# A 32-byte spacer above the right-hand tiles of a two-layer decoder trunk

## The chip, the cores and the metric

The kernel runs on one core of a Trainium2 chip. The metric is the device time of one execution in microseconds (us). A core has a matrix engine (TensorE; PE in the profile, with its weight loads shown apart as PEld), a vector engine (DVE), a scalar engine (ACT), a general engine (POOL), a queue engine (SP) that here issues nearly all transfers, an on-chip memory of 128 partitions (SBUF), and an accumulator memory in banks that the matrix engine writes (PSUM). A matrix multiplication takes two operands from SBUF: the stationary one is loaded into the array first (LDWEIGHTS), the moving one is then streamed through it (MATMUL).

## The reference

A trunk of two layers works on a sequence of 256 tokens with 1024 features, float32. Layer 0 mixes tokens with a gated linear recurrence, layer 1 with sparse attention of 16 heads; after each mixer comes an MLP of width 4096, and before every part a root-mean-square normalisation.

```python
for i in range(DEPTH):                         # DEPTH = 2
    h = _rmsnorm(x, norm_mix[i])
    if i % N_MIXERS == 0:
        x = x + _rglru_mixer(h, rg_w_in[j], ...)
    else:
        x = x + _nsa_mixer(h, nsa_w_in[j], ...)
    h = _rmsnorm(x, norm_ffn[i])
    x = x + _sq_relu_mlp(h, mlp_w_up[i], mlp_w_down[i])   # relu(h @ up)**2 @ down
return _rmsnorm(x, norm_final)
```

Nearly all the arithmetic is in the products with weights: the input and output projections of both mixers and the two MLPs.

## The kernel before

**Layout.** The activations stand transposed: features on the partitions, tokens along a row, in chunks of 128 features by 256 tokens (1024 bytes a partition). `xt` is the residual stream. A weight matrix is cut into pieces of 128 x 1024, which is eight stationary operands of 128 x 128.

**Precision by splitting.** A product in float32 is made of three in the faster type float32r. A weight piece arrives in a `raw` tile; ACT (now and then DVE) writes its rounded high part to a `whi` tile (L278 in the MLPs, L326 in the planned sections), and DVE writes the difference raw minus high to a `wlo` tile (L287 and L323). The activations are split in the same way into pairs: `hhl` holds the normalised input (high and low part of eight chunks), `uhl` the MLP's activations (32 tiles, one for each chunk of 128 of the width 4096), `xbh`/`xbl` the recurrence's output, `oh`/`ol` the attention's. `mm3` (L317 to L320) then does high times high, high times low and low times high into one PSUM bank. The weight is stationary, the activation moves, so each of the three matmuls has its own weight load of 128 x 128 and streams 256 columns.

**Stages.** The recurrence layer (L525 to L764) and the attention layer (L828 to L1247) are planned: a list scheduler in Python (`Plan`) with written costs gives each engine its order of instructions before the kernel is built. The two MLPs (`mlp`, L766 to L819) are written out: 32 up-projections read `hhl` and write `uhl`, 8 down-projections read `uhl`, and `tick` splits later weight pieces in between. In the attention layer the value projection (`values`, L991 to L1021) has it the other way round: `hhl` is stationary there, and `whi`/`wlo` move, in 304 and 256 columns. The scores (L1098, L1099) and the products with the probabilities (L1147, L1162) have small operands of their own.

**Loads.** SP issues the weight pieces in a fixed order into five `raw` tiles, well ahead of the splits; at the start of the recurrence layer two more pieces go to the tile `y`, which is free then (`spare`).

**Where the tiles lie.** SBUF is allocated as two stacks. Most pools grow upward from the left: `consts`, `xres`, `weights` (seven `whi`, seven `wlo`), `stats`, and then the pools of the stage. Three pools take from the right end downward: `hsplit` (the tile `hhl`), then `rawweights` (five `raw` tiles), then, during an MLP, `up0` or `up1` (`uhl`). Every tile is rounded up to a multiple of 32 bytes of a partition. As the program is allocated, `hhl` starts at byte 212960 of each partition, the `raw` tiles at 190560 + 4480 i, the `uhl` tiles 2048 bytes apart from 125024; `whi` starts at 28704 + 4480 i, `wlo` at 60064 + 4480 i. Every one of these is 32 past a multiple of 64, and so are `xbh`, `xbl`, `oh`, `ol`, `warm`, `xt`'s chunks, `t`, `u`, `sa`, `sb`, `kh`, `kl`, and the start of `pT`. Counted in blocks of 128 bytes, `hhl`, `raw`, `uhl`, `xbh`, `xbl`, `oh` and `ol` start at 96, `whi` and `wlo` at 32. Some unused tiles named `edge`, `edge0` and `edge1` (320, 64 and 64 bytes) stand in the left stack and set such positions.

The lines that the change touches are L471 to L475, where the tiles of the constants end and `hhl` is made:

```python
471    consts.tile([P, 80], F32, name="edge")
472    ones = consts.tile([P, 1], F32, name="ones")
473    pool.memset(ones, 1.0)
474    hhl = hpool.tile([P, KC, 2, S], F32R, name="hhl")
475    hh, hl = hhl[:, :, 0], hhl[:, :, 1]
```

Of the kernel before, what the change touches and what calls it, by code (L numbers as in the profile page):

```python
# [12 lines left out]
F32 = mybir.dt.float32  # L13
# [6 lines left out]
P = 128  # L20
# [199 lines left out]
def trunk_kernel(ctx: ExitStack, tc: tile.TileContext, x_in, vec_in, const_in, w2_in, wts, out):  # L220
# [6 lines left out]
    hpool = ctx.enter_context(tc.tile_pool(name="hsplit", bufs=1, side="right"))  # L227
# [243 lines left out]
    consts.tile([P, 80], F32, name="edge")  # L471
    ones = consts.tile([P, 1], F32, name="ones")
    pool.memset(ones, 1.0)
    hhl = hpool.tile([P, KC, 2, S], F32R, name="hhl")
    hh, hl = hhl[:, :, 0], hhl[:, :, 1]  # L475
    acc = spool.tile([P, S], F32, name="acc")
# [921 lines left out]
```

## Time and profile before

| | us |
|---|---|
| device time, median of 3 runs (570.91 to 571.75) | 571.49 |
| device time of the profiled execution | 571.1 |
| its span, first to last instruction | 569.3 |
| PE busy | 560.9 |
| PEld busy | 553.7 |
| DVE busy | 407.0 |
| ACT busy | 342.7 |
| POOL busy | 40.1 |
| mean granted clock of TensorE | 0.996 |

The profiled execution takes 1.8 us more than its span, for what lies before the first and after the last instruction that the profile shows. A MATMUL's busy time in the profile runs from its start to the end of its passage through the array, and the next one starts before that; so the mean of one (some 277 ns) says little, and the distance from start to start, or a count of matmuls in a stretch of time, says how fast they follow each other.

### The profile page before, as it was taken

To read this page: it belongs to the slowest core of one execution; us is meant where nothing else is said; L and a number is where in the kernel's file an instruction comes from. 1 tells how busy PE (TensorE), PEld (TensorE's weight loads), DVE (VectorE), ACT (ScalarE), POOL (GpSimd) and SP (SyncE) were. 2 spreads that over 40 slices of the span, in tenths; PEclk is the share of its full clock that TensorE was granted. 3 is DMA by queue.
4 is the path that set the end of the run, shared out by engine and by line. 5 is a ranking of instruction groups with operands and counts; after the bars stand their busy time and mean duration, and the time that the engine had idled before them with its cause. 6 is when DMAs were issued, how large, how long until landed. Compare 5 with 4: busy or idle time off the path is not lost.

```text
span 569.3 us, 12420 instructions
## 1 busy us (share of the span) xinstructions
PE 560.9 (99%) x4906; PEld 553.7 (97%) x4906; DVE 407.0 (71%) x877; ACT 342.7 (60%) x666; POOL 40.1 (7%) x55
## 2 busy tenths in 40 slices
PE   9999999999999999999999999999999999999995
PEld 8989999999999999999999999999999999999995
DVE  6999989766775664565749999989867775553532
ACT  7799675865664443444456988886865664443410
POOL 1000000000000211221000000000000000222310
PEclk9999999999999999999999999999999999999998
DMA  8936468556657456456685232354676666566402
GB/s 318 407 98 209 121 214 255 184 189 191 195 194 235 155 204 222 163 190 221 212 264 154 65 114 57 112 171 144 198 230 193 191 202 231 156 205 218 126 1 74
DMA packets 33225, 103.66 MB, mean 182 GB/s; under 512 B 3856, under 2 KB 8080, under 8 KB 33168
## 3 DMA queue, kind: packets, MB, share of 16 engines
q1 hardware_dynamic: 32624, 102.42, 55.8%
q8 instruction: 38, 0.62, 0.4%
q10 hardware_dynamic: 544, 0.46, 0.2%
q14 instruction: 19, 0.16, 0.1%
HBM read 99.23 MB, written 1.05 MB: 176 GB/s over the span
## 4 chain that ended last, share of the span: by engine, by line
PE 95%; DVE 2%; issue 1%; DMA 1%; ACT 1%; DVEq 0%; POOL 0%; SPq 0%; ACTq 0%; POOLq 0%
PE bank L318 28%; PE bank L319 27%; PE bank L320 27%; PE bank L1162 3%; PE bank L686 2%; PE bank L1147 2%; PE bank L1098 1%; PE bank L1099 1%; PE bank L567 1%; DMA pt<-tt 1%; PE bank L1005 1%; DVE wlo L323 1%; PE bank L1006 1%; PE bank L1007 1%; ACT whi L326 1%
## 5 line engine op out<-in xcount | busy, mean ns | idle before, releaser
L318 PE MATMUL bank<-hhl,whi 128*128 128x256 f32 x768 | 213.2, 278 | 0.0
L319 PE MATMUL bank<-hhl,whi 128*128 128x256 f32 x768 | 212.4, 277 | 0.0
L320 PE MATMUL bank<-hhl,wlo 128*128 128x256 f32 x768 | 212.2, 276 | 0.0
L287 DVE TENSOR_TENSOR wlo<-raw,whi 128x1024 fp32r<-128x1024 f32 x115 | 143.2, 1266 | 1.9 <-ACT whi L278 1.9
L319 PEld LDWEIGHTS bank<-hhl,whi 128*128 128x128 f32 x768 | 144.3, 188 | 0.3 <-DVE hhl L576 0.2
L318 PEld LDWEIGHTS bank<-hhl,whi 128*128 128x128 f32 x768 | 144.3, 188 | 0.1
L320 PEld LDWEIGHTS bank<-hhl,wlo 128*128 128x128 f32 x768 | 144.2, 188 | 0.0
L318 PE MATMUL bank<-uhl,whi 128*128 128x256 f32 x512 | 141.5, 276 | 0.0
L319 PE MATMUL bank<-uhl,whi 128*128 128x256 f32 x512 | 141.4, 276 | 0.0
L320 PE MATMUL bank<-uhl,wlo 128*128 128x256 f32 x512 | 141.4, 276 | 0.0
L278 ACT CAST whi<-raw 128x1024 fp32r<-128x1024 f32 x116 | 118.1, 1039 | 23.1 <-issue 18.8
L318 PEld LDWEIGHTS bank<-uhl,whi 128*128 128x128 f32 x512 | 96.1, 188 | 0.0
L319 PEld LDWEIGHTS bank<-uhl,whi 128*128 128x128 f32 x512 | 96.1, 188 | 0.0
L320 PEld LDWEIGHTS bank<-uhl,wlo 128*128 128x128 f32 x512 | 96.1, 188 | 0.0
L323 DVE TENSOR_TENSOR wlo<-raw,whi 128x1024 fp32r<-128x1024 f32 (+2 forms) x72 | 77.4, 1091 | 7.0 <-ACT whi L326 6.9
L326 ACT CAST whi<-raw 128x1024 fp32r<-128x1024 f32 (+2 forms) x63 | 60.0, 966 | 21.4 <-PE bank L319 9.1
L522 DVE TENSOR_TENSOR xt<-xt,bank 128x256 f32<-128x256 f32 x39 | 15.9, 418 | 75.8 <-PE bank L320 75.8
L783 ACT ACTIVATE u<-t 128x256 f32<-128x256 f32 x64 | 26.7, 418 | 58.8 <-DVE t L778 58.6
L778 DVE SCALAR_TENSOR_TENSOR t<-bank,rstd 128x256 f32<-128x256 f32 x64 | 26.9, 423 | 39.7 <-PE bank L320 39.5
L1112 ACT ACTIVATE pt<-pt,mx 128x256 f32<-128x256 f32 (+1 forms) x64 | 28.7, 450 | 3.6 <-DVE mx L1109 3.2
L785 DVE TENSOR_TENSOR uhl<-u,uhl 128x256 fp32r<-128x256 f32 x64 | 26.6, 416 | 3.0 <-ACT uhl L784 3.0
L498 ACT ACTIVATE hhl<-xt,vec 128x256 fp32r<-128x256 f32 x8 | 4.1, 510 | 39.4 <-DVE xt L522 39.4
(201 smaller groups left out, 730.5 us busy)
## 6 DMA issues: line engine op xcount, KB each, us to landing
raw<-in_dram SPq DMA_DIRECT2D x171, 512.0 KB, 4.4
raw<-in_dram SPq DMA_DIRECT2D x4, 560.0 KB, 4.7
gw<-in_dram SPq DMA_DIRECT2D x4, 512.0 KB, 8.3
raw<-in_dram SPq DMA_DIRECT2D x6, 256.0 KB, 5.2
y<-in_dram SPq DMA_DIRECT2D x2, 512.0 KB, 6.8
pT<-in_dram SPq DMA_DIRECT2D x2, 512.0 KB, 5.7
xt<-in_dram SPq DMA_DIRECT2D x3, 256.0 KB, 5.2
kh<-kh SPq DMA_DIRECT2D x8, 64.0 KB, 2.8
```

Source lines behind the costliest of these rows:

```text
L278: (act.copy if eng is None else eng.tensor_copy)(hi_t[i % NSPL][:, :n], raw_of(i)[:, :n])
L287: (eng or dve).tensor_tensor(lo[:, :n], raw_of(i)[:, :n], hi[:, :n].bitcast(F32), op=OP.subtract)
L318: pe.matmul(ps, wh, xh, start=start, stop=False)
L319: pe.matmul(ps, wh, xl, start=False, stop=False)
L320: pe.matmul(ps, wl, xh, start=False, stop=stop)
L323: return lambda e: e.tensor_tensor(o, a, h.bitcast(F32), op=OP.subtract)
L326: return lambda e: (e.copy if e is act else e.tensor_copy)(o, a)
L778: dve.scalar_tensor_tensor(t, z, 0.0, rs, op0=OP.max, op1=OP.mult)
L783: act.activation(u, t, AF.Square)
L785: later(lambda: dve.tensor_tensor(ul[m], u, uh[m].bitcast(F32), op=OP.subtract))
L1112: add("act", (0.39, 0.49)[qc], lambda e, row=row, j=j: e.activation(row, row, AF.Exp, bias=mx[:, j:j + 1], scale=-1.0, accum_out=sm[:, j:j ...
L1162: two = lambda c, w, y, **k: [e.matmul(o()[own_(hf), c0 + c.start:c0 + c.stop], w(hf), y(hf), **k) for hf in range(2)]
```

## The change

One tile is added to the pool `hsplit` ahead of `hhl`: 8 float32 values, 32 bytes of each partition, which nothing reads or writes. As the pool takes from the right end downward, the new tile lies above `hhl`, and `hhl`, the five `raw` tiles and the 32 `uhl` tiles of each MLP lie 32 bytes lower: `hhl` at 212928, `raw` at 190528 + 4480 i, `uhl` from 124992, all at multiples of 64 (64 past a multiple of 128). The left stack, with `whi`, `wlo`, `xt`, `xbh`, `xbl`, `oh`, `ol` and all others, does not move. No instruction is added, removed or reordered; the scheduler does not see addresses, so the order on every engine and all waits stay as they are.

```diff
     consts.tile([P, 80], F32, name="edge")
     ones = consts.tile([P, 1], F32, name="ones")
     pool.memset(ones, 1.0)
+    hpool.tile([P, 8], F32, name="edge2")
     hhl = hpool.tile([P, KC, 2, S], F32R, name="hhl")
     hh, hl = hhl[:, :, 0], hhl[:, :, 1]
     acc = spool.tile([P, S], F32, name="acc")
```

## The prediction

> **What bounds the kernel now.** I read the page first: busy times, granted clock, and the chain that ended last by engine and line.
>
> ```profile
> PE 560.9 (99%) x4906; PEld 553.7 (97%) x4906; DVE 407.0 (71%) x877; ACT 342.7 (60%) x666; POOL 40.1 (7%) x55
> PEclk9999999999999999999999999999999999999998
> PE 95%; DVE 2%; issue 1%; DMA 1%; ACT 1%; DVEq 0%; POOL 0%; SPq 0%; ACTq 0%; POOLq 0%
> PE bank L318 28%; PE bank L319 27%; PE bank L320 27%; PE bank L1162 3%; PE bank L686 2%; PE bank L1147 2%; PE bank L1098 1%; PE bank L1099 1%; PE bank L567 1%; DMA pt<-tt 1%; PE bank L1005 1%; DVE wlo L323 1%; PE bank L1006 1%; PE bank L1007 1%; ACT whi L326 1%
> ```
>
> The matrix engine at its full clock is the bound: 82% of the chain are the three lines of `mm3`, 95% some matmul. No wait of it is worth removing; only the pace of the matmuls is. So the next view was the groups by line and shape, for how many of them read a moved tile, then the windows, for their pace in two stretches without a pause. (A windows row: stretch, its length, PE busy with the count, clock, DMA share, GB/s.)
>
> ```profile
> L318 PE MATMUL bank<-hhl,whi 128*128 128x256 f32 x768 | 213.2, 278 | 0.0
> L318 PE MATMUL bank<-uhl,whi 128*128 128x256 f32 x512 | 141.5, 276 | 0.0
> L318 PE MATMUL bank<-oh,whi 128*128 128x256 f32 x64 | 18.4, 288 | 0.0
> L318 PE MATMUL bank<-xbh,whi 128*128 128x256 f32 x64 | 17.7, 276 | 0.0
> ...
> 110.00:210.00 100.00, 100.00 (x883) 1.00 0.62 195
> 400.00:540.00 140.00, 140.00 (x1238) 1.00 0.62 195
> ```
>
> `hhl` moves in 3 x 768 = 2304 matmuls and `uhl` in 3 x 512 = 1536: 3840 of 4906 stream a tile that the change shifts. `oh` and `xbh` stay. A window also counts the matmuls under way at its edge, 0.276 us long, about 2.4 of them; so the pace is 140 / 1235.6 = 0.1133 us from start to start. One nanosecond of it is worth 3.84 us.
>
> What is 113.3 ns made of? The timeline gives the price of a column, where the value projection streams 304 and then 256:
>
> ```profile
> 284.05 0.31 PE L1005 MATMUL bank<-whi,hhl 128*128 128x304 f32 x1
> 284.19 0.30 PE L1006 MATMUL bank<-wlo,hhl 128*128 128x304 f32 x1
> 284.33 0.30 PE L1007 MATMUL bank<-whi,hhl 128*128 128x304 f32 x1
> 284.47 0.28 PE L1005 MATMUL bank<-whi,hhl 128*128 128x256 f32 x1
> 284.59 0.28 PE L1006 MATMUL bank<-wlo,hhl 128*128 128x256 f32 x1
> 284.71 0.28 PE L1007 MATMUL bank<-whi,hhl 128*128 128x256 f32 x1
> ```
>
> Three of 304 take 0.42 us, 140 ns each; two of 256 take 0.24 us, 120 ns each. 20 ns for 48 columns is 0.417 ns a column, 106.7 ns for 256. In the steady stretches a matmul therefore takes 6.6 ns more than its columns, and 6.6 / 0.417 is 16 columns, which is 64 bytes of float32. A row of 1024 bytes that starts 32 past a multiple of 64 touches 17 blocks of 64 bytes; one that starts on a multiple touches 16. 17 x 16 columns x 0.417 ns is 113.3 ns. That is the case for the change.
>
> The other candidate is the weight load, since each matmul has its own. Its pace alone shows where the moving operand is one column wide (L514), and its place in the steady rhythm beside it:
>
> ```profile
> 19.59 0.53 PEld L514 LDWEIGHTS bank<-ones,x 128*128 128x128 f32 x4
> 20.04 0.19 PEld L318 LDWEIGHTS bank<-hhl,whi 128*128 128x128 f32 x1
> 20.15 0.19 PEld L319 LDWEIGHTS bank<-hhl,whi 128*128 128x128 f32 x1
> ...
> 300.34 0.28 PE L318 MATMUL bank<-hhl,whi 128*128 128x256 f32 x1
> 300.35 0.19 PEld L319 LDWEIGHTS bank<-hhl,whi 128*128 128x128 f32 x1
> 300.46 0.28 PE L319 MATMUL bank<-hhl,whi 128*128 128x256 f32 x1
> ```
>
> Five loads start in 20.15 - 19.59 = 0.56 us, 112 ns apiece. In the rhythm a load starts some 0.01 us after a matmul has started, and the next matmul 0.11 us after the load. The load is thus close behind: however fast the stream becomes, the loads alone hold the pace near 112 ns.
>
> Last, the rhythm is not always kept:
>
> ```profile
> 6.09 1.11 PE L567 MATMUL bank<-warm 128*128 128x256 f32 x8
> 7.04 0.28 PE L318 MATMUL bank<-hhl,whi 128*128 128x256 f32 x1
> ...
> 8.42 0.28 PE L318 MATMUL bank<-hhl,whi 128*128 128x256 f32 x1
> ...
> 9.84 0.28 PE L318 MATMUL bank<-hhl,whi 128*128 128x256 f32 x1
> 9.95 0.28 PE L319 MATMUL bank<-hhl,whi 128*128 128x256 f32 x1
> ```
>
> From 8.42 to 9.84 are twelve matmuls, 118 ns each, on the same tiles that later run at 113.3; eight on `warm` take 0.95 us, 119 ns each. Stream and load disturb each other there, and fall into step from 9.84 on. That step is something the change can spoil.
>
> **The change part by part.** No instruction and no wait is added or moved; three kinds of access get another start address.
>
> (1) `hhl` and `uhl` as the moving operand, 3840 matmuls. The bounds: nothing gained if the load holds 113.3 already; at the other end the columns alone, 6.6 ns x 3840 = 25.3 us, which the load's own pace forbids. Between these I take the load's 112 ns, the nearest row: 113.3 - 112 = 1.3 ns, times 3840 = 5.0 us. What is late next is the load, whose tiles `whi` and `wlo` stay where they are. Stretches out of step get no term.
>
> The Trainium skill ("TensorE: Matmul & The Clock Gate", section "Wait — 56ns, not 53.3ns?") puts the warm distance at N / 2.4 GHz plus about 2.5 ns; for 256 columns that is an estimate of 109.2 ns, 4.1 ns under this trace. By it the sum would be 4.1 x 3840 = 15.7 us. The trace's 113.3 ns departs from it, so part of the 6.6 ns is not that fixed cost.
>
> (2) `raw` as a source of the splits, and `hhl`, `uhl` as their target. Price of an element:
>
> ```profile
> L323 DVE TENSOR_TENSOR wlo<-raw,whi 128x1024 fp32r<-128x1024 f32 x56 | 67.7, 1219 | 6.9 <-ACT whi L326 6.9
> L323 DVE TENSOR_TENSOR wlo<-raw,whi 128x256 fp32r<-128x256 f32 x12 | 4.6, 421 | 0.0
> L705 DVE SCALAR_TENSOR_TENSOR t<-a,t 128x512 f32<-128x512 f32 x4 | 2.7, 686 | 0.1
> L702 DVE SCALAR_TENSOR_TENSOR i<-i,xb 128x512 f32<-128x512 f32 x4 | 2.7, 683 | 0.0
> ...
> 263.59 1.03 ACT whi L326
> 283.26 1.22 DVE wlo L323
> ```
>
> (1219 - 421) / 768 = 1.04 ns an element. `a` (L705) lies on a multiple of 64, everything at L702 32 past one: 686 against 683 ns, no gain. I take zero. Were a 64-byte block saved or lost per split it would be 16 x 1.04 = 17 ns; in the MLPs that is hidden by the matmuls, and between 263.6 and 284.5 us (the last two rows, of the chain in order of time), where the chain leaves PE, seven splits stand on it: 0.12 us either way. Without the cover, 180 splits would cost 3 us.
>
> (3) The loads into `raw`, all on SP's queue.
>
> ```profile
> raw<-in_dram SPq DMA_DIRECT2D x171, 512.0 KB, 4.4
> ACT whi L326 <- DMA raw<-in_dram: 4.0, 7, 1.2
> ```
>
> A split waits for a load seven times, 4.0 us in all. One block of 64 in a row of 4096 bytes is 1/64 of 4.4 us, 0.07 us, seven times 0.5 us either way; I take zero, as the same bytes move in the same number of rows.
>
> (4) `hhl` as the stationary operand, 96 matmuls of the value projection, at 120 and 140 ns, not in step: between -5 and +5 ns each, 0.5 us either way, taken as zero.
>
> The sum: 571.1 (the profiled execution) - 5.0 = 566.1. The median of the runs is 0.4 above the profiled one: **566.5 us**.
>
> **The rivals.** *Faster, as above* (A): for it speaks the exact 17 x 16, and that columns are the slope; against it, that the load is so close. Its own range, for a pace between 111.4 and 112.9 ns, is 564 to 570.
>
> *No change* (B): the 113.3 is a closed loop of matmul start, load start, 0.11 us, next matmul start; the moving address has no part in it. The rows at 300.34 to 300.46 fit this as well. For it speaks that the loads at 19.59 are only 1.3 ns faster with almost no stream beside them; against it, that 304 columns take 20 ns longer than 256, so the stream does count. Time: 571.5, with (2) to (4) between 570.4 and 572.6. The Trainium skill ("SBUF — State Buffer", section "Door 1: The DMA port swizzle") gives SBUF lines of 16 bytes; both starts are on such a line and a row has 64 lines either way, so by that rule the result is this one. No row here shows lines of 16.
>
> *Slower* (C): the step is lost. The stream now changes block half a block earlier against the weights, which still start in the middle of one, and the two may meet at the memory in every matmul, as between 8.42 and 9.84. Price 118 - 113.3 = 4.7 ns for each one out of step: it decides from 1.14 us / 4.7 ns = 243 more of them, costs 9.0 us for half of the 3840 (580.5) and 18.0 for all (589.5). For it speaks that the same tiles run at both paces; against it, that every long stretch did find its step.
>
> *Much faster* (D): load and hand-over overlap, so that only the 0.11 us from load to matmul is left, 110 ns: 3.3 x 3840 = 12.7 us, 558.8. Against it the 112 at L514.
>
> **How the numbers follow.** A 0.40, B 0.30, C 0.24, D 0.06. The predicted time is A's. A change of 0.2%, 1.1 us, is about what a measurement of this kernel can tell from none. Faster by more: A and D, 0.46; the same: B, 0.30; slower: C, 0.24. The range goes from 558 (D) to 581 (C with half of the matmuls out of step); left out are C's worse half and what lies below D, about 0.13. A's own range stands above.
>
> **What would show it.** The stretch 110 to 210 holds 883 matmuls: near 893 for A, 883 for B, 848 if C is complete, 909 for D. The distance from load to matmul stays 0.11 us in A and B and grows under C. The loads at L514 stay at 112 ns, DVE's 1219 ns and ACT's splits stay within 20 ns, or (2) was wrong. The prediction is wrong if the pace changes where `oh` or `xbh` stream, which did not move, or if the time changes while the pace in that stretch doesn't.

## The result, and the profile after

| | before | after |
|---|---|---|
| device time, median (range) | 571.50 us (570.91 to 571.75) | **577.73 us** (577.50 to 578.52) |
| runs | 4 | 4 |
| ratio after / before, 95% interval | | 1.0123 (1.0110 to 1.0137) |
| span of the profiled execution | 569.3 us | 575.7 us |
| mean granted clock | 0.996 | 0.997 |

The change makes the kernel 6.2 us slower; 566.5 us, faster, was forecast. Each engine's busy time, the chain by engine, and the group with the most matmuls, of the profile page after:

```profile
PE 567.7 (99%) x4906; PEld 560.9 (97%) x4906; DVE 407.0 (71%) x877; ACT 343.1 (60%) x666; POOL 40.1 (7%) x55
PE 95%; DVE 2%; issue 1%; ACT 1%; DMA 1%; DVEq 0%; POOL 0%; SPq 0%; ACTq 0%; POOLq 0%
L318 PE MATMUL bank<-hhl,whi 128*128 128x256 f32 x768 | 213.1, 277 | 0.0
```

Same counts, same clock, same bound; only PE and its loads (PEld, 553.7 before) are busy longer, by 6.8 and 7.2 us, and a group's busy time hides where. The windows show it. They are laid inside the four MLP stages: up-projections of layer 0, down-projections of layer 0, then the same two of layer 1. Columns: stretch, length, PE busy with the count of matmuls, clock, DMA share, GB/s. Before:

```profile
110.00:170.00 60.00, 60.00 (x531) 1.00 0.62 194
185.00:260.00 75.00, 75.00 (x664) 1.00 0.57 192
410.00:470.00 60.00, 60.00 (x532) 1.00 0.68 207
490.00:555.00 65.00, 65.00 (x576) 1.00 0.45 144
```

and after:

```profile
110.00:170.00 60.00, 60.00 (x532) 1.00 0.64 196
185.00:260.00 75.00, 75.00 (x634) 1.00 0.55 179
410.00:470.00 60.00, 60.00 (x532) 1.00 0.69 209
490.00:555.00 65.00, 65.00 (x553) 1.00 0.49 154
```

With 2.4 taken off each count for the matmuls at the edges, the pace of the up-projections (`hhl` streams) is 113.3 ns before and after (the 531 gives 113.5; one matmul more or less in 60 us is 0.2 ns). The down-projections (`uhl` streams) go from 75 / 661.6 = 113.4 to 75 / 631.6 = 118.7 ns in layer 0 and from 113.3 to 65 / 550.6 = 118.1 ns in layer 1. Times 768 matmuls each that is 4.1 + 3.6 = 7.7 us. The span grew by 6.4; the other 1.3 us are small gains elsewhere, 0.5 of them reached before 20 us (the same load starts at 20.04 us in the prediction's row and at 19.54 after, shown further down) and 0.7 in the attention layer. The timeline of the layer 0 down-projections, PE alone, first before:

```profile
199.72 0.28 PE L319 MATMUL bank<-uhl,whi 128*128 128x256 f32 x1
199.83 0.28 PE L320 MATMUL bank<-uhl,wlo 128*128 128x256 f32 x1
199.95 0.28 PE L318 MATMUL bank<-uhl,whi 128*128 128x256 f32 x1
...
200.74 0.28 PE L319 MATMUL bank<-uhl,whi 128*128 128x256 f32 x1
```

and after:

```profile
199.82 0.28 PE L318 MATMUL bank<-uhl,whi 128*128 128x256 f32 x1
199.94 0.28 PE L319 MATMUL bank<-uhl,whi 128*128 128x256 f32 x1
200.06 0.28 PE L320 MATMUL bank<-uhl,wlo 128*128 128x256 f32 x1
200.18 0.28 PE L318 MATMUL bank<-uhl,whi 128*128 128x256 f32 x1
...
200.89 0.28 PE L318 MATMUL bank<-uhl,whi 128*128 128x256 f32 x1
```

Before, nine matmuls start in 1.02 us, 113 ns each; after, nine in 1.07 us, 119 ns each, all three lines alike. PE is busy throughout both windows. The pace after is the one called out of step in the prediction.

**A premise was wrong.** The text on the change and the prediction say that `hhl` moves. It does not. A right-hand pool ends where the pool before it began, but inside it the tiles are laid upward: the five `raw` tiles lie at 190560 + 4480 i, the first the lowest. By that order `edge2`, made first, takes the low 32 bytes of `hsplit`, 212928 to 212960, and `hhl` stays at 212960. Only the pools to its left, `raw` and `uhl`, lie 32 lower. That `hhl`'s stages keep 113.3 ns to the count agrees, and a run below moves `hhl` itself.

### The profile page after: what moved, and what is told of

It is laid out like the page before. It is cut to its first block, busy times and chain, and to the rows that moved or that the text cites. A ratio compares the mean times of both kernels' runs of the same rounds, so it can differ in the third digit from the quotient of the medians.

```text
span 575.7 us, 12420 instructions
## 1 busy us (share of the span) xinstructions
PE 567.7 (99%) x4906; PEld 560.9 (97%) x4906; DVE 407.0 (71%) x877; ACT 343.1 (60%) x666; POOL 40.1 (7%) x55
## 4 chain that ended last, share of the span: by engine, by line
PE 95%; DVE 2%; issue 1%; ACT 1%; DMA 1%; DVEq 0%; POOL 0%; SPq 0%; ACTq 0%; POOLq 0%
PE bank L318 28%; PE bank L319 27%; PE bank L320 27%; PE bank L1163 3%; PE bank L687 2%; PE bank L1148 2%; PE bank L1099 1%; PE bank L1100 1%; PE bank L568 1%; DMA pt<-tt 1%; PE bank L1006 1%; DVE wlo L323 1%; PE bank L1007 1%; PE bank L1008 1%; ACT whi L326 1%
## 5 line engine op out<-in xcount | busy, mean ns | idle before, releaser
L319 PE MATMUL bank<-uhl,whi 128*128 128x256 f32 x512 | 144.1, 281 | 0.0
L318 PE MATMUL bank<-uhl,whi 128*128 128x256 f32 x512 | 144.0, 281 | 0.0
L320 PE MATMUL bank<-uhl,wlo 128*128 128x256 f32 x512 | 144.0, 281 | 0.0
```

Of the source, the lines that this page charges most:

```text
L318: pe.matmul(ps, wh, xh, start=start, stop=False)
L319: pe.matmul(ps, wh, xl, start=False, stop=False)
L320: pe.matmul(ps, wl, xh, start=False, stop=stop)
```

## The experiments

Three theories stood at first. **Blocks**: the moving row's start decides alone; by the prediction a start on a multiple of 64 is better, by T2 of the expectations it is worse. **T3**: the new place of `raw` disturbs the matmuls. **Distance** (T1, from rival C): what counts is where the moving row starts against the stationary operand, from which the step of stream and load depends. Before, `hhl` and `uhl` start at 96 and the weights at 32 in blocks of 128 bytes, a distance of 64; after, `uhl` stands at 64, a distance of 32. Further runs ask how exact the distance must be, whether the length of the load plays a part, and whether fewer, wider streams escape it. Diffs are against the kernel before unless told otherwise. Kernels with an interval ran several times; the others ran once, beside before.

**Which tile does it.** `uhl_only` moves the activations alone 32 bytes lower, `raw_only` the weights' landing tiles alone (`uhl` then lies 2048 lower than before, a whole number of blocks).

```diff
# uhl_only, in mlp behind the uhl tiles
+            up.tile([P, 8], F32, name="pad")
# raw_only, against the kernel after, behind the uhl tiles
+            up.tile([P, 504], F32, name="pad")
```

> Only uhl lies 32 bytes lower, at 64 past a multiple of 128; raw and hhl lie as before. Theory T1 (what counts is how the start of the moving row stands to the start of the weights): the down-projections lose the step, 118 to 119 ns a matmul against 113.3, the up-projections keep it; 577 to 578 us. T2 (a moving row that starts on a multiple of 64 is slow by itself): the same. T3 (raw's new place makes the splits or loads collide with the matmuls): 571 to 572 us.

> Only raw lies 32 bytes lower; uhl lies 2048 bytes lower than before, so again 96 past a multiple of 128. T1 and T2: as before, 571 to 572 us, every long stretch at 113.3 ns. T3: 577 to 578 us, with the down-projections at 118 to 119 ns.

Measured: `uhl_only` 577.54 us, ratio 1.0125 (1.0108 to 1.0142); `raw_only` 571.03, 1.0007 (0.9996 to 1.0019). The down-projection windows, first of `uhl_only`:

```profile
185.00:260.00 75.00, 75.00 (x634) 1.00 0.55 180
490.00:555.00 65.00, 65.00 (x552) 1.00 0.46 153
```

and of `raw_only`:

```profile
185.00:260.00 75.00, 75.00 (x664) 1.00 0.59 191
490.00:555.00 65.00, 65.00 (x576) 1.00 0.45 146
```

Both pads stand behind the `uhl` tiles in the program; as the tiles of a right-hand pool are laid upward, such a pad lies above them and pushes them down. The 32 bytes by which `uhl` lies lower are the whole loss; `raw` is worth nothing, and T3 falls.

**Row or distance.** `as_described` does what the section on the change says: a spacer behind `hhl`, so that `hhl`, `raw` and `uhl` all lie 32 lower. `all_lower` lowers the left stack by 32 as well, weights included: every operand then starts on a multiple of 64, and the distance is 64 again.

```diff
# as_described
     hhl = hpool.tile([P, KC, 2, S], F32R, name="hhl")
+    hpool.tile([P, 8], F32, name="pad_h")
# all_lower: the same, and
-    consts.tile([P, 80], F32, name="edge")
+    consts.tile([P, 72], F32, name="edge")
```

> hhl, raw and uhl all lie 32 bytes lower: here the normalised input moves too. T1 and T2: the up-projections and the projections of both mixers lose the step as well, up to 2304 more matmuls at 5.4 ns, 585 to 591 us. T3: 577 to 578 us, the up-projections at 113.3 ns. The theory of the prediction (fewer blocks in an aligned row) has the up-projections at 112 ns.

> Everything lies 32 bytes lower, the weights whi and wlo too, so every address of before has lost 32 and all differences are as before; all tiles of the big matmuls start on a multiple of 64. T1: the step is back everywhere, 571 to 572 us at 113.3 ns. T2: all stages are slow, 590 us or more. The theory of blocks: less than 113.3 ns, 560 to 567 us.

Measured: `as_described` 587.81 us, ratio 1.0305 (1.0290 to 1.0321); `all_lower` 570.57, 1.0004 (0.9994 to 1.0013). The windows of `as_described`:

```profile
110.00:170.00 60.00, 60.00 (x508) 1.00 0.55 187
185.00:260.00 75.00, 75.00 (x637) 1.00 0.57 190
410.00:470.00 60.00, 60.00 (x508) 1.00 0.61 187
490.00:555.00 65.00, 65.00 (x553) 1.00 0.57 186
```

and of `all_lower`:

```profile
110.00:170.00 60.00, 60.00 (x532) 1.00 0.58 195
185.00:260.00 75.00, 75.00 (x664) 1.00 0.58 193
410.00:470.00 60.00, 60.00 (x532) 1.00 0.68 203
490.00:555.00 65.00, 65.00 (x576) 1.00 0.43 140
```

With `hhl` moved, its stages fall to 60 / 505.6 = 118.7 ns too. With everything on a multiple of 64 the pace is 113.3 to the count, neither faster nor slower. So the row's own start costs and brings nothing; the theory of blocks falls, both as gain and as loss.

**How exact the distance must be.** Four kernels, with another distance in each stage. `sweep_64_96` lowers `uhl` by 64 in layer 0 and by 96 in layer 1. `weights_96` puts the kernel after's weights 96 higher, so that `uhl` is 64 away from them again and `hhl` 96. `fine_16` and `fine_8` go 16 and 8 bytes to either side of 64.

```diff
# sweep_64_96, behind the uhl tiles
+            up.tile([P, (16, 24)[layer]], F32, name="pad")
# weights_96, against the kernel after, ahead of the first weight tile
+    wpool.tile([P, 24], F32, name="pad_w")
# fine_16; fine_8 has (2, 30)
+            ub = up.tile([P, NF * 2 * S + 32], F32R, name="uhl")
+            uo = (4, 28)[layer]
+            uhl = [ub[:, uo + 2 * S * i:uo + 2 * S * (i + 1)] for i in range(NF)]
```

> From the kernel before: uhl 64 bytes lower in layer 0 (32 past a multiple of 128, the same place in a block of 64 as the weights) and 96 bytes lower in layer 1 (on a multiple of 128). If the relation to the weights repeats every 64 bytes, layer 0's down-projections keep 113.3 to 113.5 ns and layer 1's run at 118 to 119, some 575 us. If it repeats only every 128 bytes, layer 0 loses the step too, 578 us or more.

> From the changed kernel: the weights (and the left tiles above them) lie 96 bytes higher, on a multiple of 128; uhl stays at 64 past one, hhl at 96 past one. T1 (the relation): the down-projections are back at 113.3 to 113.5 ns, since uhl and the weights stand to each other as before, and now the up-projections, with hhl in the middle of a block and the weights at its start, run at 118 to 119; oh and xbh moved with the weights. If the start of the moving row alone counted, down stays at 118 to 119 and up at 113.3.

> From the kernel before: uhl 16 bytes higher in layer 0 and 16 bytes lower in layer 1. If the two streams only have to be in the same half of a block of 64, both layers keep 113.3 to 113.5 ns (571 us); if their starts have to agree exactly, both run at 118 to 119 (578 us). The theory of blocks has no gain here.

> From the kernel before: uhl 8 bytes higher in layer 0 and 8 bytes lower in layer 1. As for 16 bytes: 113.3 to 113.5 ns in both layers if a neighbourhood is enough, 118 to 119 if the starts have to agree exactly; an intermediate pace would say that the loss grows with the distance.

One run each: 579.31, 581.29, 579.14 and 580.49 us beside 570.78 of before. All four windows of `weights_96`, where one kernel holds both cases:

```profile
110.00:170.00 60.00, 60.00 (x506) 1.00 0.55 186
185.00:260.00 75.00, 75.00 (x664) 1.00 0.58 193
410.00:470.00 60.00, 60.00 (x505) 1.00 0.60 186
490.00:555.00 65.00, 65.00 (x576) 1.00 0.52 170
```

The loss has changed sides: the down-projections of the kernel after, with nothing done to `uhl`, are back at 664 and 576, and the up-projections, whose `hhl` did not move, pay. The down-projections of `sweep_64_96` and of `fine_8`:

```profile
185.00:260.00 75.00, 75.00 (x634) 1.00 0.54 178
490.00:555.00 65.00, 65.00 (x550) 1.00 0.49 155
```

```profile
185.00:260.00 75.00, 75.00 (x623) 1.00 0.53 176
490.00:555.00 65.00, 65.00 (x545) 1.00 0.48 154
```

Put together, from these counts (`fine_16` counts 631 and 552 there), less 2.4:

| moving start less stationary start, modulo 128 | where | ns from start to start |
|---|---|---|
| 0 | `sweep_64_96`, layer 0 | 118.7 |
| 32 | after, down, layers 0 and 1; `as_described`, up | 118.7, 118.1; 118.7 |
| 48 | `fine_16`, layer 1 | 118.3 |
| 56 | `fine_8`, layer 1 | 119.8 |
| **64** | before, `raw_only`, `all_lower`; `weights_96`, down | **113.3 to 113.5** |
| 72 | `fine_8`, layer 0 | 120.9 |
| 80 | `fine_16`, layer 0 | 119.3 |
| 96 | `sweep_64_96`, layer 1; `weights_96`, up | 118.7; 119.1, 119.4 |

Of these eight distances the step is kept at 64 alone. It is no slope: eight bytes to either side lose more than 32 do. One thing was not kept apart there: `fine_8`'s rows start at 104 and 120, the only starts here that are no multiple of 16, so the 1.5 to 1.6 ns by which it is slower than `fine_16` may come from the row's own start and not from the distance.

**Does the load's length set the pace?** The prediction held that the loads alone allow no less than 112 ns. `half_load` loads 64 of the 128 weight columns in most down-projections, `quarter_load` 32; the other output features of these chunks are left out. Each keeps the distance of 64 in one layer (`uhl` 128 lower) and has 32 in the other. `half_load`; `quarter_load` has 32 columns and the two pads exchanged:

```diff
# behind the uhl tiles
+            up.tile([P, (32, 8)[layer]], F32, name="pad")
...
-                        mm3(z, wh[:, w], wl[:, w], uh[i], ul[i], i == 0 and not seeded, i == NF - 1)
+                        if seeded or i in (0, NF - 1):
+                            mm3(z, wh[:, w], wl[:, w], uh[i], ul[i], i == 0 and not seeded, i == NF - 1)
+                        else:
+                            c = slice(k * P, k * P + 64)
+                            mm3(z[:64], wh[:, c], wl[:, c], uh[i], ul[i], False, i == NF - 1)
```

> From the kernel before: in the down-projections all but the first and the last of the 32 chunks load only 64 of the 128 weight columns (the other 64 output features of those chunks are left out; the last output chunk of layer 1 is done in full), so the weight load is half as long while the stream stays 256 columns. uhl stands to the weights as before in layer 0 and 32 bytes lower in layer 1, as in the changed kernel. Theory L (the chain matmul start, load, next matmul start sets the 113.3 ns): layer 0's down-projections fall to 107 to 110 ns. Theory S (the stream itself takes 16 columns more): layer 0 stays at 113.3. If the loss of the step is stream and load meeting in the memory, layer 1 still loses by it but less than 5 ns against layer 0; if the load is hardly needed for it, the difference stays 5 ns.

> As the run with half the weight columns, but with 32 of 128 (the other 96 output features of chunks 2 to 31 are left out), and uhl 32 bytes lower in layer 0, 128 lower in layer 1. If the stream loses time only while a load reads the memory beside it, layer 0 loses a quarter of the 5.4 ns, 114.5 to 115; if the loss does not hang on the length of the load, layer 0 stays near 118. Layer 1 stays at 113.3, whatever the length of the load.

One run each: 574.59 us beside a median of 570.67, and 572.60 beside 570.89. From `half_load`, the group of short loads and the two windows (the first at distance 64, the second at 32):

```profile
L318 PEld LDWEIGHTS bank<-uhl,whi 128*64 128x64 f32 x450 | 60.4, 134 | 0.0
...
185.00:260.00 75.00, 75.00 (x664) 1.00 0.59 191
490.00:555.00 65.00, 65.00 (x553) 1.00 0.45 145
```

and from `quarter_load` (the first at 32, the second at 64):

```profile
L318 PEld LDWEIGHTS bank<-uhl,whi 128*32 128x32 f32 x450 | 48.8, 108 | 3.4
...
185.00:260.00 75.00, 75.00 (x640) 1.00 0.55 184
490.00:555.00 65.00, 65.00 (x574) 1.00 0.45 147
```

The busy time of a load falls from 188 ns to 134 and to 108. In step the pace is the same as with the full load, 664 and 574 against 664 and 576. Out of step half a load saves nothing (553 against 553), a quarter load about 1 ns (75 / 637.6 = 117.6). So neither the 113.3 ns nor the loss of 5 ns is the time that a load takes.

**Fewer, wider streams.** High and low part of a chunk of `uhl` lie side by side. `wide_down` streams both, 512 columns, through one loaded high weight and 256 through the low weight, with one more addition at the end of each output chunk; that is two loads a chunk instead of three. The last output chunk of layer 1 stays as it was. `wide_down_after` is the same on the kernel after; `wide_both` does it in the up-projections too.

```diff
-                z = next(zrot)[:, :S]
+                zw = next(zrot)
+                z = zw[:, :S]
...
-                        mm3(z, wh[:, w], wl[:, w], uh[i], ul[i], i == 0 and not seeded, i == NF - 1)
...
+                            pe.matmul(zw, wh[:, w], uhl[i], start=i == 0, stop=False)
+                            pe.matmul(z, wl[:, w], uh[i], start=False, stop=False)
...
+                        residual(zw[:, S:], m)
```

> From the kernel before: in the down-projections high and low part of uhl, which lie side by side, are streamed in one matmul of 512 columns against whi, and the low weights get their own of 256: two loads a chunk instead of three; one more addition of 128 x 256 for each of the 15 output chunks done so. L: 216 + 113 = 329 ns a chunk against 340, 566 to 568 us. S: 220 + 113 = 333 ns, 567.5 to 569 us. If neither, the pair takes 340 and the time stays at 571.

> The same edit on the changed kernel, with uhl 32 bytes lower. If every matmul whose load overlaps a stream out of step pays some 5 ns, two are left to pay of three: 10 ns a chunk over the run with the wide stream alone, some 5 us more than it. If the wide stream leaves the load room enough, the difference to it is under 2 us.

> As the wide stream in the down-projections, and the same for 29 of the 32 up-projections of each MLP, where ACT copies the second half out of PSUM and DVE adds the halves before what was done before. Another 464 chunks at 7 to 11 ns less: 3.2 to 5 us under the run with the down-projections alone, 562 to 565 us, if ACT and DVE keep up; if they don't, the pace of the up-projections goes over 340 ns a chunk.

Measured: `wide_down` 576.71 us, ratio 1.0109 (1.0087 to 1.0131); `wide_down_after` 578.33 (one run, beside 570.67); `wide_both` 579.47, 1.0159 (1.0135 to 1.0183). The timeline of `wide_down`, PE in the layer 0 down-projections:

```profile
199.80 0.39 PE L817 MATMUL bank<-uhl,whi 128*128 128x512 f32 x1
200.03 0.28 PE L818 MATMUL bank<-uhl,wlo 128*128 128x256 f32 x1
200.15 0.39 PE L817 MATMUL bank<-uhl,whi 128*128 128x512 f32 x1
...
201.19 0.39 PE L817 MATMUL bank<-uhl,whi 128*128 128x512 f32 x1
```

Four chunks in 1.39 us, 348 ns each, where three matmuls in step take 340: some 231 ns for 512 columns and 117 for 256. At 0.417 ns a column the first is 17 ns above its columns, the second 11. In step, 6.6 each would make 333. That the step is lost here is read from this pace; it fits that the distance no longer matters: the two windows of the down-projections hold 431 and 375 matmuls in `wide_down`, 432 and 374 in `wide_down_after`. The distance of 64 is thus needed and not enough, as the rows of the prediction from 8.42 to 9.84, `hhl` at distance 64 and 118 ns, say too. 480 chunks at 8 ns are 3.8 of `wide_down`'s 6.0 us; the rest was not traced to a cause. The up-projections of `wide_both` go no faster: 346 matmuls in 60 us, 349 ns a chunk. The saved load brings nothing, which fits the half loads. As a price, estimated from these rows: out of step about 6.6 + 5.4 ns above the columns for each 256 of them, 5.4 more for the second 256.

**Only one weight off.** Is it a matmul's own weights that must be 64 away, or those being loaded beside it? `lo_only` puts `wlo` 32 higher and leaves `whi`.

```diff
# ahead of the low weight tiles
+    wpool.tile([P, 8], F32, name="pad_w")
```

> From the kernel before: only the tiles wlo of the weights lie 32 bytes higher (and the left tiles above them, oh and xbh among them); whi, hhl and uhl stay. Of the three matmuls of a product, the third (L320 of the kernel before) reads wlo itself, and during the second (L319) the load of wlo runs. If a stream is disturbed by the load that runs beside it, the second takes some 118 ns and the others 113.3; if by its own weights, the third; if the rhythm as a whole is lost, all three, 590 us or so.

One run: 584.97 us beside 570.89. From the timeline of its layer 0 down-projections, PE alone:

```profile
199.88 0.28 PE L319 MATMUL bank<-uhl,whi 128*128 128x256 f32 x1
200.00 0.28 PE L320 MATMUL bank<-uhl,whi 128*128 128x256 f32 x1
200.11 0.28 PE L321 MATMUL bank<-uhl,wlo 128*128 128x256 f32 x1
200.23 0.28 PE L319 MATMUL bank<-uhl,whi 128*128 128x256 f32 x1
...
201.17 0.28 PE L321 MATMUL bank<-uhl,wlo 128*128 128x256 f32 x1
```

Eleven steps in 1.29 us, 117 ns each. The mean alone does not decide: were both guesses true together, the second and third at 118.7 and the first at 113.3 would give 116.9. But the start times in the trace, kept to the nanosecond, between 185 and 260 us put 117.4 ns behind the first, 117.0 behind the second and 118.3 behind the third. The first, which reads and runs beside `whi` alone, is slow too: one weight tile out of place takes the rhythm of all three.

## Why the prediction was wrong, point by point

**What bounds the kernel: right.** PE at its full clock, pace the only lever; the loss of the kernel after follows from counts in the four windows, but for the 1.3 us named above.

**The premise: wrong.** `hhl` was said to move. So 1536 matmuls were shifted, not 3840. The addresses of the `raw` tiles, ascending in a right-hand pool, had this in them, and they were not read for it. The effect is limited to size: `as_described`, with the premise made true, is slower still, by 3.0%.

**Term (1): the step that failed.** It read 6.6 ns as a seventeenth block of 64 bytes that an aligned row would save, and gave stretches out of step no term. The block fitted because it had been chosen to fit: one equation, one free number. `all_lower` has every row on a multiple of 64 and keeps 113.3, so no block was there to be saved. The term put at nothing decided: in place of -5.0 us the moving operand's new start brought +7.7 (1536 matmuls at some 5 ns), because its distance to the weights went from 64 to 32. What the 6.6 ns in step are is open.

**The floor of 112 ns: not what holds the pace.** It came from L514, a place with almost no stream. The loads there take the same after:

```profile
19.09 0.53 PEld L515 LDWEIGHTS bank<-ones,x 128*128 128x128 f32 x4
19.54 0.19 PEld L318 LDWEIGHTS bank<-hhl,whi 128*128 128x128 f32 x1
19.65 0.19 PEld L319 LDWEIGHTS bank<-hhl,whi 128*128 128x128 f32 x1
```

five in 0.56 us, as before; but half the load leaves 113.3 where it was. Whether 112 would hold a faster stream is open, as no stream of 256 columns was faster.

**Term (2) and (3), `raw`: right.** The split of the kernel after, and its wait for a load:

```profile
L323 DVE TENSOR_TENSOR wlo<-raw,whi 128x1024 fp32r<-128x1024 f32 x56 | 67.7, 1220 | 7.0 <-ACT whi L326 6.9
...
ACT whi L326 <- DMA raw<-in_dram: 3.7, 7, 1.1
```

1220 against 1219 ns, 3.7 against 4.0 us; `raw_only` is within 0.2% of before. **Term (4)** has no object, as `hhl` stayed.

**The rivals.** C has the right sign and the right relation ("against the weights, which still start in the middle of one"), and its 4.7 ns for a matmul out of step was close to the 5 measured; that the two "meet at the memory" is not shown, and a load half as long lost no less. Its 9.0 us for "half of the 3840" stood near 7.7 by luck of the count, which was 1536. It got 0.24, and the argument against it, "every long stretch did find its step", was the fault: all long stretches of before have the same distance, so they were one observation, not many. B's closed loop is refuted: the moving address does count. D did not occur; no run shows a stretch of 256 columns under 113 ns.

**Two rules cited in the prediction.** By the Trainium skill's rule of 16-byte lines ("SBUF — State Buffer", section "Door 1: The DMA port swizzle"), both of `uhl`'s starts are alike; the pace here differs by 5 ns, so that rule does not account for it. By the Trainium skill's distance of N / 2.4 GHz plus about 2.5 ns ("TensorE: Matmul & The Clock Gate", section "Wait — 56ns, not 53.3ns?") the estimate was 109.2 ns; no stage of any run here reached it with 256 columns.

**The checks named in the prediction.** The time from a load to the next matmul was to grow under C, and does: 0.11 us before, 0.12 in the down-projections after (load at 200.06, matmul at 200.18). 848 matmuls in 110 to 210 us were to show C complete. The window after holds 870: it mixes some 64 us of up-projections, untouched, with 36 of down-projections. A window across two stages, one moved and one not, answers neither; the ones above lie within one stage each.

## What to carry to other kernels

Before costing a shift, print the addresses that it leaves and see which operands moved; a spacer may land on the other side of the tile it was meant for. Where a matmul streams while the next weights load, look at the start of the moving row less the start of the stationary one, and try that distance in steps (here modulo 128 only 64 of eight tried was good); bringing both to multiples of 64 showed nothing. Measure pace by counts in windows that lie inside one stage, since the busy time of one matmul hides it.

## What the runs showed that was not expected

- The distance acts as a lock, not as a slope: 113.3 ns at 64, 118 to 121 at 0, 32, 48, 56, 72, 80 and 96, the worst being the two nearest to 64 (with rows that also start off a multiple of 16). It is worth 1.2% of the kernel for `uhl` and 3.0% for `hhl` and `uhl`.
- The length of a load is nearly free beside a 256-column stream: 188, 134 and 108 ns of load give the same 113.3 to 113.7 ns in step, and 118.1, 118.1 and 117.6 out of it (layer 1 twice, then layer 0, where the full load has 118.7).
- A stream twice as wide loses the step at the good distance: 348 ns for a chunk with two loads, 340 with three.
- **Open**: how stream and load disturb each other, why the good distance is 64 and repeats with 128, and what the 6.6 ns are that remain in step. The runs show the relation, not its cause; no kernel faster than before was found.
